# A two-layer attention encoder: three multiplications of branch attention placed on other engines

## The chip, the core and the metric

The kernel runs on one core of one Trainium2 chip. The core has TensorE (PE, matrix products into PSUM), VectorE (DVE), ScalarE (ACT), GpSimd (POOL) and SyncE (SP, which issues the weight loads). Each engine works through its own queue in order and waits on semaphores for the others. The metric is the device time of one execution in microseconds (us).

## The reference

A batch of one sequence of 512 tokens, width 1024, passes two equal layers. Cut to what matters here:

```python
h = rms_norm(x, norm_mix)
qa, ka, va, qb, kb, vb, qc, kc, vc, gate_logits = split(h @ w_in)
qa, ka = (apply_rope(rms_norm(t, gain), ang_1d) for t in (qa, ka))   # 4 heads of 64
qb, kb = (apply_rope(rms_norm(t, gain), ang_2d) for t in (qb, kb))   # 8 query heads, 2 key heads
qc, kc = rms_norm(qc, qk_gain[2, 0]), rms_norm(kc, qk_gain[2, 1])    # 4 heads, no rotation
oa = dilated_mixture_attention(qa, ka, va)        # softmax over masked scores
ob = gqa_block_attention(qb, kb, vb)              # softmax over all 512 keys
oc = neighborhood_attention_2d(qc, kc, vc, rpb)   # softmax over near keys, with a bias
merged = sum(sigmoid(gate) * (o @ w_branch))      # over the three branches
x = x + merged @ w_out
x = x + ffn(rms_norm(x, norm_ffn))                # up, depthwise conv, gelu gate, down
```

`apply_rope` makes `[x1 cos - x2 sin, x1 sin + x2 cos]` of the two halves of a head. The scores are scaled by 1/8.

## The kernel before, in words

All data is float32. A product of two float32 matrices is made of three passes on PE over high and low parts: a number is cast to the type fp32r (the high part, a cast on ACT) and the difference is the low part (a subtraction on DVE). Each weight granule (128 x 512) is loaded by SP and split in this way, `whi` on ACT at line 104 and `wlo` on DVE at line 106; three buffers of each are in turn. `mm3` (lines 117 to 120) makes the passes for outputs that stand feature by feature, `token_group` (lines 156 to 158) for outputs token by token. A granule feeds twelve matmuls.

A layer projects queries and keys of C (`Qc`), then the values, the keys of B (`Qk`) and the queries of B (`Qb`), gates, and later the queries and keys of A (`Qa`). `headnorm` normalises a projection head by head: squares on ACT, sums on DVE, a reciprocal root in a few small DVE steps, and a multiplication of each block of 128 tokens on DVE (line 302), after which `finish` runs. For A and B `finish` is `rotate`: two products of swapped halves with the sine table into `m` on POOL (line 316), a product with the cosine table (line 322) and a sum (line 325) on DVE. For C it is `gain_c`, a product with the gains on POOL (line 537). In A and B the gains are in the tables.

Attention works on one head and one block of 128 queries at a time. `turned` transposes two heads' queries or keys on PE (line 345), `q_stack` and `k_stack` make high and low parts of them (`qT`, `kh`, `kl`; lines 352, 353, 362, 364). `scores` multiplies (lines 378 and 379), takes the maximum on DVE (line 387, or with the bias added in line 390), the exponential and its sum on ACT (388 or 394), and on DVE the reciprocal of the sum (396) and the scaling of the probabilities `p` by it (397). `turn` transposes `p` on PE (409) and splits it, `th` on ACT (413) and `tl` on DVE (414). `values` multiplies by the values (426, 427). Three PSUM buffers are shared by scores, transposes and results of this part.

`weave` sets the attention steps of one branch between the projections and gates of the others, so that PE has matmuls to do while a block's chain runs on DVE and ACT: C's heads stand among the projections of values and `Qb`, B's among gates, C's output and `Qa`, A's among B's output and gates. The order within each engine's queue is made by a scheduler from the program's order and from priorities: `soon` and `urgent` put the chain and the copies out of PSUM ahead, `next_w` the splits of the weights ahead of both. The last part of a layer, output projection and feed-forward, has no attention in it.

## Time and profile before

| | |
|---|---|
| three runs, median (lowest to highest) | 1665.42 us (1664.78 to 1666.51) |
| the profiled execution, own time | 1666.58 us |
| its span, first to last instruction | 1664.8 us |
| TensorE's granted clock, mean over the span | 0.999 of full speed |
| PE busy | 1625.6 us (98%) |
| DVE busy | 1163.5 us (70%) |
| ACT busy | 782.5 us (47%) |
| POOL busy | 153.3 us (9%) |

The span of the profiled execution is what the views of the trace divide up; 1.8 us of its own time lie around it. A busy PE is not a PE at its peak, since matmuls overlap: one of 512 columns is shown as 0.39 us and the next starts 0.23 us after it. Idle time of PE is thus the time in which not even the tail of a matmul runs. `L397` is line 397 of the kernel; a buffer's name stands before the arrow and what it is made of behind it.

### The profile page before, as it was taken

The page shows a single profiled execution, that of the slowest core. Times are in us where ns is not written, and L with a number is a line of the kernel's source. Part 1 is how long each engine was busy: PE and PEld are TensorE (multiplying, and loading weights), DVE is VectorE, ACT ScalarE, POOL GpSimd, SP SyncE. Part 2 cuts the span into 40 slices and gives each one's busy share as a digit, 9 for nine tenths or more (in the row PEclk, how much of TensorE's full clock was granted, in tenths as well). Part 3 has the DMA queues.
Part 4 walks back from the last instruction along what each step waited for, and adds up shares of the span by engine and source line. Part 5 has one row for each costly group of instructions (what it writes and reads, how often), then busy time and mean ns, then how long its engine had stood idle before and what let it go on. Part 6 is the DMA issues. An engine that isn't in the chain of part 4 may idle for free.

```text
span 1664.8 us, 21596 instructions
## 1 busy us (share of the span) xinstructions
PE 1625.6 (98%) x7697; PEld 1340.9 (81%) x7697; DVE 1163.5 (70%) x2110; ACT 782.5 (47%) x1424; POOL 153.3 (9%) x150
## 2 busy tenths in 40 slices
PE   8999999999999999999999999999999999999999
PEld 6777888787888888888876778887878888888887
DVE  7898778866677734776388987788575677357753
ACT  5556565554454423444245566655543444234431
POOL 2220012203000000000031200122020000000000
PEclk9999999999999999999999999999999999999999
DMA  5222122222333333333332221222223333333333
GB/s 191 81 84 65 63 70 66 69 65 91 97 92 101 95 98 98 96 95 102 95 107 80 85 66 61 70 71 63 71 89 98 98 96 96 97 99 95 97 100 101
DMA packets 80092, 147.78 MB, mean 89 GB/s; under 512 B 8913, under 2 KB 10065, under 8 KB 79985
## 3 DMA queue, kind: packets, MB, share of 16 engines
q1 hardware_dynamic: 77184, 140.54, 27.3%
q10 hardware_dynamic: 2736, 5.74, 1.1%
q8 instruction: 60, 0.98, 0.2%
q14 instruction: 48, 0.39, 0.1%
q0 software_dynamic: 64, 0.12, 0.0%
HBM read 144.28 MB, written 2.10 MB: 88 GB/s over the span
## 4 chain that ended last, share of the span: by engine, by line
PE 84%; DVE 10%; issue 2%; ACT 2%; POOL 1%; DMA 1%; SPq 0%; DVEq 0%; ACTq 0%; POOLq 0%
PE acc L118 23%; PE acc L120 23%; PE acc L119 23%; PE acc L156 3%; PE acc L158 3%; PE acc L157 3%; DVE wlo L106 2%; PE tpp L409 2%; PE s L378 2%; PE s L379 1%; PE po L427 1%; PE po L426 1%; DVE p L397 1%; DVE tl L414 1%; DVE p L390 1%
## 5 line engine op out<-in xcount | busy, mean ns | idle before, releaser
L106 DVE TENSOR_TENSOR wlo<-raw,whi 128x512 fp32r<-128x512 f32 x520 | 378.6, 729 | 403.7 <-ACT whi L104 314.5
L104 ACT CAST whi<-raw 128x512 fp32r<-128x512 f32 x520 | 322.0, 620 | 556.8 <-PE acc L119 411.3
L118 PE MATMUL acc<-xh,whi 128*128 128x512 f32 x1152 | 452.3, 393 | 0.0
L120 PE MATMUL acc<-xh,wlo 128*128 128x512 f32 x1152 | 449.7, 390 | 0.0
L119 PE MATMUL acc<-xl,whi 128*128 128x512 f32 x1152 | 449.1, 390 | 0.0
L120 PEld LDWEIGHTS acc<-xh,wlo 128*128 128x128 f32 x1152 | 216.2, 188 | 45.4
L119 PEld LDWEIGHTS acc<-xl,whi 128*128 128x128 f32 x1152 | 216.4, 188 | 44.4
L118 PEld LDWEIGHTS acc<-xh,whi 128*128 128x128 f32 x1152 | 216.3, 188 | 43.7
L118 PE MATMUL acc<-gh,whi 128*128 128x512 f32 x384 | 149.4, 389 | 0.0
L119 PE MATMUL acc<-gl,whi 128*128 128x512 f32 x384 | 149.4, 389 | 0.0
L120 PE MATMUL acc<-gh,wlo 128*128 128x512 f32 x384 | 149.4, 389 | 0.0
L156 PE MATMUL acc<-whi,xh 128*128 128x512 f32 (+1 forms) x320 | 120.4, 378 | 4.1 <-ACT whi L104 1.5
L157 PE MATMUL acc<-wlo,xh 128*128 128x512 f32 (+1 forms) x320 | 119.5, 373 | 1.4 <-DVE wlo L106 1.4
L158 PE MATMUL acc<-whi,xl 128*128 128x512 f32 (+1 forms) x320 | 119.0, 372 | 0.7 <-DVE xl L186 0.7
L689 ACT ACTIVATE cv<-us,params 128x512 f32<-128x512 f32 x96 | 75.6, 811 | 31.8 <-DVE us L687 31.8
L413 ACT CAST th<-tpp 128x512 fp32r<-128x512 f32 (+2 forms) x128 | 69.7, 544 | 32.7 <-PE tpp L409 28.4
L118 PEld LDWEIGHTS acc<-gh,whi 128*128 128x128 f32 x384 | 72.1, 188 | 15.0
L120 PEld LDWEIGHTS acc<-gh,wlo 128*128 128x128 f32 x384 | 72.1, 188 | 15.0
L119 PEld LDWEIGHTS acc<-gl,whi 128*128 128x128 f32 x384 | 72.1, 188 | 14.9
L414 DVE TENSOR_TENSOR tl<-tpp,th 128x512 fp32r<-128x512 f32 (+2 forms) x128 | 81.0, 634 | 2.5 <-ACT th L413 1.9
L409 PE MATMUL tpp<-ident,p 128*128 128x128 f32 x464 | 72.9, 275 | 6.0 <-DVE tl L414 2.3
L156 PEld LDWEIGHTS acc<-whi,xh 128*128 128x128 f32 x320 | 60.7, 190 | 15.3 <-ACT whi L104 2.2
(149 smaller groups left out, 2339.4 us busy)
## 6 DMA issues: line engine op xcount, KB each, us to landing
raw<-w SPq DMA_DIRECT2D x520, 256.0 KB, 2.6
x_all<-xT SPq DMA_DIRECT2D x8, 256.0 KB, 5.4
bias_a<-bias_a ACTq DMA_DIRECT2D x4, 512.0 KB, 4.4
out<-x_all SPq DMA_DIRECT2D x8, 256.0 KB, 2.6
T<-rpb ACTq DMA_DIRECT2D x8, 192.0 KB, 2.8
rope_raw<-rope ACTq DMA_DIRECT2D x4, 256.0 KB, 3.7
gn<-gains ACTq DMA_DIRECT2D x2, 384.0 KB, 4.1
params<-small ACTq DMA_DIRECT2D x1, 232.0 KB, 4.0
```

Of the source, the lines that this page charges most:

```text
L104: nc.scalar.copy(hi, src)
L106: nc.vector.tensor_tensor(out=lo, in0=src, in1=hi.bitcast(F32), op=ALU.subtract)
L118: nc.tensor.matmul(ps, lhsT=lh, rhs=rh, start=first, stop=False)
L119: nc.tensor.matmul(ps, lhsT=lh, rhs=rl, start=False, stop=False)
L120: nc.tensor.matmul(ps, lhsT=ll, rhs=rh, start=False, stop=last)
L156: nc.tensor.matmul(o, lhsT=xh[:, t], rhs=wh[:, c], start=k == 0, stop=False)
L157: nc.tensor.matmul(o, lhsT=xh[:, t], rhs=wl[:, c], start=False, stop=False)
L158: nc.tensor.matmul(o, lhsT=xl[:, t], rhs=wh[:, c], start=False, stop=k == KD - 1)
L409: nc.tensor.transpose(tp[:, i * 128 : (i + 1) * 128], p[:, i * 128 : (i + 1) * 128], ident)
L413: nc.scalar.copy(hd["th"][sl], v_)
L414: nc.vector.tensor_tensor(out=hd["tl"][sl], in0=v_, in1=hd["th"][sl].bitcast(F32), op=ALU.subtract)
L689: nc.scalar.activation(out=t, in_=us, func=AF.Identity, scale=cw[:, 1, j : j + 1], bias=cb[:, j : j + 1])
```

## The change

Three things are done otherwise.

1. `gain_c` is gone. The small parameters get two more columns for each layer, the gains of C's queries and keys. One DVE call for each layer makes their product times -0.125 (`g_c`), and `q_stack` multiplies C's transposed queries by it while it splits them: ACT's copy gets a column of scales, DVE's subtraction becomes a multiply-and-subtract. The keys of C get no gain of their own any more.
2. In `rotate` the two products of swapped halves are made on DVE. There are 48 in the run: 32 of 128x256 for `Qa` and `Qb`, 16 of 128x64 for `Qk`.
3. The scaling of `p` by the reciprocal sum is an ACT copy with a column of scales. There are 128.

```diff
--- before.py
+++ after.py
@@ -22,7 +22,7 @@
 KF = DFF // 128
 EPS = 1e-6
 BIG = 1e30
-NSMALL = 3 * 48 + 48 + 24 + 8 + 8
+NSMALL = 3 * 48 + 48 + 24 + 8 + 8 + 2
 
 
 
@@ -243,6 +243,11 @@
         g_ffn = sm[:, 224:232]
         nc.vector.tensor_scalar(out=bg, in0=bg, scalar1=0.5, scalar2=None, op0=ALU.mult)
 
+        g_c = sm[:, 232:233]
+        nc.vector.scalar_tensor_tensor(
+            out=g_c, in0=g_c, scalar=-0.125, in1=sm[:, 233:234], op0=ALU.mult, op1=ALU.mult
+        )
+
         with ExitStack() as actx:
             at = actx.enter_context(tc.tile_pool(name=f"att{l}", bufs=1, reuse_waits="tile"))
             xh, xl, split = normed(x, g_mix, "A", res)
@@ -257,7 +262,7 @@
                     nc.scalar.dma_start(
                         out=gn.rearrange("p a b c d -> p (a b c d)"), in_=gains[l : l + 1, :].to_broadcast([128, 768])
                     )
-                for br, s in ((0, -0.125), (1, 0.125), (2, -0.125)):
+                for br, s in ((0, -0.125), (1, 0.125)):
                     nc.vector.tensor_scalar(
                         out=gn[:, br, 0], in0=gn[:, br, 0], scalar1=s, scalar2=None, op0=ALU.mult
                     )
@@ -313,7 +318,7 @@
                 mv = m[:, :w_].rearrange("p (s h d) -> p s h d", s=ns, d=64)
                 Qv = Q.rearrange("p (s h d) -> p s h d", s=ns, d=64)
                 for a, b in ((0, 32), (32, 0)):
-                    nc.gpsimd.tensor_tensor(
+                    nc.vector.tensor_tensor(
                         out=mv[:, :, :, a : a + 32],
                         in0=Qv[:, :, :, b : b + 32],
                         in1=table(1)[:, :, None, a : a + 32].to_broadcast([128, ns, nh, 32]),
@@ -345,12 +350,21 @@
                     nc.tensor.transpose(tp[:, b * 128 : (b + 1) * 128], Q[:, b, c : c + 128], ident)
                 return tp
 
-            def q_stack(tp, odd):
+            def q_stack(tp, odd, gain):
 
                 qT = at.tile([128, 512], F32R, tag="qT", bufs=3, name=nm("qT"))
                 src = tp[64 * odd : 64 * odd + 64, :]
-                nc.scalar.copy(qT[0:64], src)
-                nc.vector.tensor_tensor(out=qT[64:128], in0=src, in1=qT[0:64].bitcast(F32), op=ALU.subtract)
+                if gain is None:
+                    nc.scalar.copy(qT[0:64], src)
+                    nc.vector.tensor_tensor(out=qT[64:128], in0=src, in1=qT[0:64].bitcast(F32), op=ALU.subtract)
+                else:
+                    nc.scalar.activation(
+                        out=qT[0:64], in_=src, func=AF.Copy, scale=gain[64 * odd : 64 * odd + 64]
+                    )
+                    nc.vector.scalar_tensor_tensor(
+                        out=qT[64:128], in0=src, scalar=gain[0:64], in1=qT[0:64].bitcast(F32),
+                        op0=ALU.mult, op1=ALU.subtract,
+                    )
                 return qT
 
             def k_stack(tp, odd):
@@ -394,7 +408,7 @@
                         nc.scalar.activation(out=p, in_=p, func=AF.Exp, bias=m, scale=-1.0, accum_out=den)
                 with soon():
                     nc.vector.reciprocal(out=rden, in_=den)
-                    nc.vector.tensor_scalar(out=p, in0=p, scalar1=rden, scalar2=None, op0=ALU.mult)
+                    nc.scalar.activation(out=p, in_=p, func=AF.Copy, scale=rden)
                 hd["p", b] = p
 
             def turn(hd, b):
@@ -457,7 +471,7 @@
                     else:
                         tp = turned(pair[0]["Q"], pair[0]["qc"])
                         for i, hd in enumerate(pair):
-                            hd["qT"] = q_stack(tp, i)
+                            hd["qT"] = q_stack(tp, i, hd["gain"])
 
                 def slot(s):
                     nxt = s // 8 * 8 + 8
@@ -532,13 +546,7 @@
 
             Qc = at.tile([128, 4, 512], F32, tag="Q", bufs=2, name=nm("Qc"))
 
-            def gain_c(b):
-                v_ = Qc[:, b].rearrange("p (s h d) -> p s h d", s=2, d=64)
-                nc.gpsimd.tensor_tensor(
-                    out=v_, in0=v_, in1=gn[:, 2, :, 0][:, :, None, :].to_broadcast([128, 2, 4, 64]), op=ALU.mult
-                )
-
-            norm_c = headnorm(Qc, 8, gain_c)
+            norm_c = headnorm(Qc, 8, lambda b: None)
 
             def ev_c(b, ps):
                 copy_q(Qc[:, b], b, ps)
@@ -577,10 +585,10 @@
                 f = bc.rearrange("p k c -> p (k c)")
                 return lambda b: (f[:, 0:256], f[:, 256:640], f[:, 256:640], f[:, 640:896])[b]
 
-            def head(h, Q, qc, K, kc, v, vh, outs, blocks=lambda b: range(4), bias=None, prep=None):
+            def head(h, Q, qc, K, kc, v, vh, outs, blocks=lambda b: range(4), bias=None, prep=None, gain=None):
                 return dict(
                     h=h, Q=Q, qc=qc, K=K, kc=kc, v=v, vh=vh, outs=outs, blocks=blocks,
-                    bias=bias, bias_prep=prep,
+                    bias=bias, bias_prep=prep, gain=gain,
                 )
 
 
@@ -598,7 +606,7 @@
             oC = []
             near = lambda b: range(max(0, b - 1), min(4, b + 2))
             heads_c = [
-                head(h, Qc, h * 64, Qc, 256 + h * 64, vC, h, oC, blocks=near, prep=lambda h=h: bias_c(h))
+                head(h, Qc, h * 64, Qc, 256 + h * 64, vC, h, oC, blocks=near, prep=lambda h=h: bias_c(h), gain=g_c)
                 for h in range(4)
             ]
             gC, gate_c = gates(2)
@@ -837,6 +845,7 @@
                 per(b_gate),
                 per(norm_mix),
                 per(norm_ffn),
+                np.concatenate([qk_gain[:, 2], qk_gain[:, 2]], axis=2).transpose(2, 0, 1),
             ],
             axis=2,
         )
```

By the added lines, lines 302, 316, 322 and 325 become 307, 321, 327 and 330; 353 becomes 364 for branch C; 390, 394, 396, 397, 413 and 414 become 404, 408, 410, 411, 427 and 428. Numbers in names only tell buffers apart, and differ by a few between the two programs.

The first place is DVE's queue in the first layer at the third block of C's first head, where its probabilities (`p_735` before; its sum's reciprocal is `rden_734`, and `rden_730` after) become ready. Before:

```order
L390 ISA p_752,m_749<-s_746,bc_534 128x256
L390 ISA m_749 128x1
L396 RECIPROCAL rden_734<-den_733 128x1
L198 TENSOR_SCALAR nx_616<-hss_183 128x8
L353 TENSOR_TENSOR qT_563<-tpq_555,qT_563 64x512
L106 TENSOR_TENSOR wlo_925<-raw_921,whi_923 128x512
L397 TENSOR_SCALAR p_735<-p_735,rden_734 128x384
L396 RECIPROCAL rden_751<-den_750 128x1
L199 TENSOR_SCALAR rq_184<-nx_616 128x8
L397 TENSOR_SCALAR p_752<-p_752,rden_751 128x256
```

Now:

```order
L404 ISA p_748,m_745<-s_742,bc_530 128x256
L404 ISA m_745 128x1
L410 RECIPROCAL rden_730<-den_729 128x1
L198 TENSOR_SCALAR nx_612<-hss_184 128x8
L199 TENSOR_SCALAR rq_185<-nx_612 128x8
L202 TENSOR_SCALAR rq_185<-rq_185 128x8
L106 TENSOR_TENSOR wlo_921<-raw_917,whi_919 128x512
L204 TENSOR_TENSOR nt_613<-rq_185 128x8
L205 SCALAR_TENSOR_TENSOR nt_613<-nt_613,nx_612 128x8
L206 SCALAR_TENSOR_TENSOR rq_185<-nt_613,rq_185 128x8
L410 RECIPROCAL rden_747<-den_746 128x1
```

The scalings of `p` have left this queue, and the reciprocal for the block after it still stands behind the `wlo` (`rden_751` before, `rden_747` now), while the one for this block keeps its place ahead of it.

The second place is ACT's queue at the same blocks (`p_735` before is `p_731` now). Before:

```order
L394 ACTIVATE p_735,den_733<-p_735,m_732 128x384
L104 CAST whi_923<-raw_921 128x512
L394 ACTIVATE p_752,den_750<-p_752,m_749 128x256
L564 DMA T_1102<-rpb 128x384
L413 CAST th_782<-tpp_784 128x3x128
L394 ACTIVATE p_796,den_794<-p_796,m_793 128x256
L104 CAST whi_967<-raw_965 128x512
L413 CAST th_782<-tpp_819 128x2x128
```

Now:

```order
L408 ACTIVATE p_731,den_729<-p_731,m_728 128x384
L104 CAST whi_919<-raw_917 128x512
L411 ACTIVATE p_731<-p_731,rden_730 128x384
L408 ACTIVATE p_748,den_746<-p_748,m_745 128x256
L572 DMA T_1098<-rpb 128x384
L411 ACTIVATE p_748<-p_748,rden_747 128x256
L427 CAST th_778<-tpp_780 128x3x128
L408 ACTIVATE p_792,den_790<-p_792,m_789 128x256
L411 ACTIVATE p_792<-p_792,rden_791 128x256
L104 CAST whi_963<-raw_961 128x512
L427 CAST th_778<-tpp_815 128x2x128
```

Behind each exponential there is now a scaling that needs the reciprocal from DVE, in two places with nothing between them, and `whi` and `th` stand behind it.

The third place is DVE's queue at the normalising and the rotation of the first two blocks of `Qb`. Before:

```order
L302 TENSOR_TENSOR Qb_185<-Qb_185,rq_187 128x512 x2
L396 RECIPROCAL rden_1196<-den_1195 128x1
L106 TENSOR_TENSOR wlo_1336<-raw_1332,whi_1334 128x512
L397 TENSOR_SCALAR p_1197<-p_1197,rden_1196 128x256
L414 TENSOR_TENSOR tl_1184<-tpp_1220,th_1183 128x2x128
L322 TENSOR_TENSOR Qb_185<-Qb_185,rope_246 128x512 x2
L390 ISA p_1231,m_1228<-s_1225,bc_1104 128x384
L390 ISA m_1228 128x1
L106 TENSOR_TENSOR wlo_1359<-raw_1355,whi_1357 128x512
L325 TENSOR_TENSOR Qb_185<-Qb_185,m_1048 128x512
```

Now:

```order
L307 TENSOR_TENSOR Qb_186<-Qb_186,rq_188 128x512 x2
L321 TENSOR_TENSOR m_1044<-Qb_186,rope_246 128x8x32
L428 TENSOR_TENSOR tl_1180<-tpp_1181,th_1179 128x3x128
L321 TENSOR_TENSOR m_1044<-Qb_186,rope_246 128x8x32
L321 TENSOR_TENSOR m_1050<-Qb_186,rope_246 128x8x32
L106 TENSOR_TENSOR wlo_1332<-raw_1328,whi_1330 128x512
L404 ISA p_1193,m_1190<-s_1187,bc_1100 128x256
L404 ISA m_1190 128x1
L327 TENSOR_TENSOR Qb_186<-Qb_186,rope_246 128x512
L321 TENSOR_TENSOR m_1050<-Qb_186,rope_246 128x8x32
L410 RECIPROCAL rden_1192<-den_1191 128x1
L428 TENSOR_TENSOR tl_1180<-tpp_1216,th_1179 128x2x128
```

The products into `m` now stand in this queue between the normalising and the cosine products, ahead of a `wlo` and of the maximum of a block of scores (line 390, now 404). On POOL the same rows are gone, and nothing else of POOL's order has changed; SP's order is the same.

## Rows read from the trace of the kernel before

**Rows 1.** The page, part 1: busy time, share, instructions by engine.

```profile
PE 1625.6 (98%) x7697; PEld 1340.9 (81%) x7697; DVE 1163.5 (70%) x2110; ACT 782.5 (47%) x1424; POOL 153.3 (9%) x150
```

**Rows 2.** Busy time by stretch: length, PE, PEld, DVE, ACT, POOL, granted clock, DMA share, GB/s.

```profile
56.00:145.00 89.00, 80.62 (x400) 62.67 (x399) 81.78 (x205) 53.67 (x121) 18.19 (x24) 1.00 0.24 76
145.00:240.00 95.00, 95.00 (x510) 80.71 (x509) 73.93 (x141) 55.53 (x112) 2.59 (x2) 1.00 0.21 64
240.00:350.00 110.00, 105.82 (x579) 88.44 (x578) 91.64 (x176) 58.96 (x117) 26.75 (x23) 1.00 0.22 68
880.00:985.00 105.00, 96.36 (x475) 75.70 (x474) 91.91 (x222) 62.23 (x137) 18.39 (x24) 0.98 0.24 73
```

**Rows 3.** Who PE waited for, 56 to 145 us: total us, times, longest.

```profile
PE s L378 <- DVE tl L414: 2.2, 4, 0.8
PE s L378 <- DVE qT L353: 1.5, 2, 0.9
PE tpp L409 <- DVE p L397: 1.4, 1, 1.4
PE acc L156 <- ACT Qk L530: 1.0, 1, 1.0
```

**Rows 4.** Timeline at 106 us (start, us; idle before), POOL, DVE, PE picked out.

```profile
106.13 4.04 POOL L316 TENSOR_TENSOR m<-Qb,rope 128x256 f32<-128x256 f32 x4 [15.67 <-ACT p L394]
...
106.55 1.16 DVE L106 TENSOR_TENSOR wlo<-raw,whi 128x512 fp32r<-128x512 f32 x1
107.64 0.82 DVE L397 TENSOR_SCALAR p<-p,rden 128x256 f32<-128x256 f32 x1
...
107.37 0.39 PE L119 MATMUL acc<-xl,whi 128*128 128x512 f32 x1
107.60 0.40 PE L120 MATMUL acc<-xh,wlo 128*128 128x512 f32 x1
108.84 0.44 PE L378 MATMUL s<-kh,qT 128*128 128x384 f32 x1 [0.84 <-DVE tl L414]
```

**Rows 5.** DVE groups (busy us, mean ns): 145 to 240, 56 to 145, 240 to 350.

```profile
L106 DVE TENSOR_TENSOR wlo<-raw,whi 128x512 fp32r<-128x512 f32 x22 | 15.2, 691 | 9.9 <-ACT whi L104 6.8 <-PE tpp L409 2.8
L397 DVE TENSOR_SCALAR p<-p,rden 128x512 f32<-128x512 f32 x23 | 11.2, 486 | 0.6
...
L106 DVE TENSOR_TENSOR wlo<-raw,whi 128x512 fp32r<-128x512 f32 x21 | 17.3, 825 | 2.3 <-ACT whi L104 2.1
L397 DVE TENSOR_SCALAR p<-p,rden 128x384 f32<-128x384 f32 x8 | 4.3, 538 | 0.0
L397 DVE TENSOR_SCALAR p<-p,rden 128x256 f32<-128x256 f32 x8 | 3.9, 488 | 0.0
L397 DVE TENSOR_SCALAR p<-p,rden 128x512 f32<-128x512 f32 x3 | 1.5, 487 | 0.1
...
L397 DVE TENSOR_SCALAR p<-p,rden 128x512 f32<-128x512 f32 x19 | 12.5, 660 | 0.4
```

**Rows 6.** Groups of the whole run, DVE and ACT, each shape apart.

```profile
L302 DVE TENSOR_TENSOR Qc<-Qc,rq 128x512 f32<-128x512 f32 x8 | 9.5, 1231 | 0.1
L325 DVE TENSOR_TENSOR Qk<-Qk,m 128x128 f32<-128x128 f32 x8 | 2.1, 281 | 0.0
...
L184 ACT ACTIVATE xh<-x_all,params 128x512 fp32r<-128x512 f32 x16 | 11.4, 717 | 2.7 <-DVE x_all L723 2.7
L331 ACT ACTIVATE vA<-acc,rcol 128x256 fp32r<-128x256 f32 x8 | 3.3, 466 | 0.0
```

**Rows 7.** Timeline of PE in the second layer at 872 us.

```profile
872.72 0.50 PE L157 MATMUL acc<-wlo,xh 128*128 128x512 f32 x1 [1.12 <-DVE wlo L106]
```

**Rows 8.** Line 397 of the whole run: who waited for it.

```profile
  PE tpp L409: 2.1, 2
```

**Rows 9.** The reciprocal of the whole run, as in rows 5.

```profile
L396 DVE RECIPROCAL rden<-den 128x1 f32<-128x1 f32 x128 | 20.5, 160 | 23.1 <-ACT p L388 12.7 <-ACT p L394 9.3
```

**Rows 10.** Who PE waited for, 240 to 350 us, as in rows 3.

```profile
PE s L378 <- ACT p L388: 1.0, 2, 0.5
```

## The prediction

> **What bounds the kernel now.** I read the page first: TensorE (PE) is busy for 98% of the span, VectorE (DVE) for 70%, ScalarE (ACT) for 47%, GpSimd (POOL) for 9% [rows 1]. A kernel of that shape gets faster only where PE stands idle, so the second view is the busy time by stretch [rows 2]. In 56 to 145 us (branch C's heads among the projections of the first layer) PE is busy for 80.62 of 89 us, so 8.38 us idle; its twin in the second layer (880 to 985) has 8.64 us idle; where branch B ends and A starts (240 to 350) it is 4.18 us, and I take as much for that place in the second layer. In pure branch B (145 to 240) there is none. The stretches with idle PE are those in which POOL works most and DVE is fullest: 81.78 of 89 us in the first, against 73.93 of 95 in B.
>
> Third, what PE waits for in 56 to 145 us [rows 3]: mostly DVE, namely `tl` (the low halves of the probabilities, whose end frees a PSUM buffer for the next scores), `qT`, and once the scaled probabilities `p`; ACT once, for a copy of `Qk`. A look at one such wait [rows 4] shows how it comes about. POOL runs four swapped products of the rotation for 4.04 us from 106.13. In that time DVE's `wlo` takes 1.16 us and a 256-wide scaling of `p` 0.82 us, and the scores that wait behind them start at 108.84. The last matmul before them started at 107.60, and matmuls else start 0.23 us apart, so this wait costs 1.01 us where the idle column says 0.84. I take every microsecond of PE's idle time as 1.2 us of span.
>
> Without that company `wlo` takes 691 ns (mean in branch B), with it 825 ns (mean in 56 to 145 us) [rows 5]. So POOL's work costs DVE time, and DVE's lateness costs PE time.
>
> **The gain on the query and key of C.** The change takes away POOL's multiplication of `Qc` by the gains (8 calls in all) and puts the product of both gains into the query stack. Beside those calls DVE's normalising of `Qc` takes 1231 ns [rows 6], about 0.54 us over an undisturbed 691 ns [rows 5], 4.3 us for the 8. PE pays for it at one place: in the second layer it waits 1.12 us for a `wlo` queued behind them [rows 7], 1.3 us by the factor above. Nothing of the kind stands in the first layer, where the projection's matmuls cover it; without that cover the same 1.3 us would be due there. The stack's new forms (a copy with a column of scales, a multiply-and-subtract) replace calls of the same size, eight pairs in the run; I put nothing on them, bounded by 0.1 us each way a call, 1 us in all. The two column products at the start stand before the first `xl` on DVE: 0 to 0.4 us, taken as 0.2. Together: -1.1 us.
>
> **The rotation.** 48 products leave POOL for DVE: 32 of 128x256 and 16 of 128x64. The trace has none on DVE. Its nearest rows are 281 ns for a 128x128 sum from SBUF [rows 6] and 691 ns for 128x512 [rows 5]; these bound the wide ones, and a line through both gives 418 ns, and 212 ns for the narrow ones (bounds 0 and 281). The C stretch holds eight of each: 3.3 + 1.7 = 5.0 us more on DVE. What DVE gets back is POOL's disturbance: 21 `wlo` at 134 ns over 691 are 2.8 us, and the eight wide products are 8 of POOL's 18.2 us there, so 1.3 us. DVE no longer waits for POOL inside a rotation, but behind the products in DVE's queue stand `wlo`, the maxima and `tl`, for which PE waits.
>
> [rows 4] shows a POOL call of about 1 us lengthening `wlo` by 0.47 us, not by its whole length. The Trainium skill, "SBUF — State Buffer" (Who interferes with whom), says that a GpSimd call and a VectorE call with two SBUF inputs exclude each other on a shared port pair for the whole instruction. By that rule DVE would get back 8 us in such a stretch and not 1.3, and the sum would be 1651; this is the third rival below.
>
> **The scaling of the probabilities.** 128 calls go from DVE to ACT. In 56 to 145 us they are 4.3 + 3.9 + 1.5 = 9.7 us of DVE [rows 5], in 240 to 350 us 12.5 us [rows 5]. On ACT the nearest row is a 128x512 copy with a column of scales from SBUF to SBUF, 717 ns [rows 6]; a 256-wide one from PSUM takes 466 ns [rows 6]. I take 717 for 512 columns and about 0.54 on average for C's 256 and 384; a block's chain gets longer by 0.23 us and a hand-over, 0.3 us. That is covered almost everywhere: of 128 scalings PE waited for two [rows 8]. If the cover were gone in all 128 it would be 38 us.
>
> The order on DVE shows one more thing: at the third block of C the scaling stood behind a `wlo`, the reciprocal ahead of it. Now only the reciprocal is needed from DVE. The wait of 1.4 us for `p` [rows 3] is the wait of that place.
>
> **The sum for PE.** How PE's waits answer to a freer DVE no row tells. I assume that idle time falls as DVE's free time grows (a queue's waits go roughly with one over its slack); bounds are nothing and all of it. In C's first stretch DVE's busy time becomes 81.8 - 9.7 + 5.0 - 1.3 = 75.8 of 89 us; the free time grows from 7.2 to 13.2, and PE's idle time falls by 45%, 3.8 us. In the second layer the same 6.0 us come off 91.9 of 105; free 13.1 becomes 19.1; 31%, 2.7 us. From B into A it is 91.6 - 12.5 + 3.3 = 82.4 of 110 (POOL's relief left out); free 18.4 becomes 27.6; 33%, 1.4 us, and as much in the second layer.
>
> That is 9.3 us idle, 11.2 us of span by the factor 1.2. Left out is TensorE's clock: its granted mean is 0.98 of full speed in C's second stretch and 1.00 in the others [rows 2]; if the shorter waits kept it up, some 2 us more would come (2% of 105), if they moved a drop into a fuller place, as much would go.
>
> Against it stands ACT. In C it takes 16 scalings at 0.54 (8.6 us) and waits in its queue for 16 reciprocals. One takes 0.16 us, and DVE stands idle 23.1/128 = 0.18 us before it [rows 9], so 0.34 us each, 5.4 us. ACT's free time of 35.3 us becomes 21.3. By the same rule PE's 1.0 us of waiting for ACT [rows 3] grows by 0.7. In B into A 19 scalings and their waits (13.6 + 6.5 us) leave 30.9 of 51.0 us, and the 1.0 us of waiting there [rows 10] grows by 0.65 in each layer. That is 2.0 us, 2.4 with the factor, and 2 x 0.3 us for the two waits for `p`: +3.0 us. Behind the waiting scaling on ACT stand `whi`, `th` and the exponentials; PE and DVE wait for these. The loads of C's bias tables are issued there too and come as much later, a head ahead of their use.
>
> In branch B the sum is 0: PE has no idle time, DVE loses 23 scalings [rows 5], and ACT goes from 55.5 [rows 2] by 23 x 0.717 to about 72 of 95 us. The merges, the feed-forward part and the DMAs aren't touched.
>
> Sum: -1.1 - 11.2 + 3.0 = -9.3 us. The profiled execution took 1666.58 us (span 1664.8 and 1.8 around it), which gives 1657.3; it was 1.2 us over the median of the runs, 1665.42, so 1656.1, rounded to 1656 us.
>
> **The rivals.** The first: ACT becomes the engine that is late, and it is slower. Each block puts 0.717 us of scaling and 0.34 us of waiting, 1.06 us, ahead of the next `th` on ACT, and `tl` follows `th`. There are some 70 blocks in the four stretches. The relief of 12.3 us (1.1 + 11.2) is used up when 12 of them reach PE; with 16 it is 17 - 12.3 = 4.7 us slower, 1670. For it: in a stretch where DVE is over 90% busy ACT waits longer than 0.34 us for a reciprocal. Against it: ACT still has 21 us free there, and 126 of 128 had slack. The Trainium skill, "ScalarE: Activation LUTs" (Rules for kernel authors), says to multiply on VectorE and not on ScalarE; the 717 against 486 ns agree with it as to the call, and by it the move alone costs. Chance 0.14.
>
> The second, hidden: PE's waits are for `tl`, and `tl` comes no earlier because `th` on ACT comes later by what DVE gains. Then only the 1.3 us at `Qc` and the 1.4 us for `p` (1.7 with the factor) go, and some 1 us comes back: 1666.6 - 2.0 - 1.2 = 1663.4. For it: DVE is 78% busy in branch B without idle PE and 83% in 240 to 350 us with 4.18 us of it [rows 2], so fullness alone isn't the cause. Chance 0.14.
>
> The third: POOL's company cost DVE its whole length, eight calls of about 1 us [rows 4]. DVE gets back 8 us a stretch: C falls to 69.0 of 89 (idle less by 64%, 5.4 us), C again to 79.1 of 105 (49%, 4.3 us), B into A to 74.4 of 110 (48%, 2.0 us, twice). That is 13.7 x 1.2 = 16.4 us, and with the other two terms -14.5: 1666.6 - 14.5 - 1.2 = 1651. With all waits on DVE gone (25.4 us idle less 3.0 that are for ACT, times 1.2, 26.9 us) it would be 1666.6 - 1.1 - 26.9 + 3.0 - 1.2 = 1640. Chance 0.11.
>
> **How the numbers follow.** My forecast (1652 to 1662) gets 0.61. What a measurement of this kernel can tell from no change is about 0.2%, 3.3 us. Faster by more: forecast, third rival and a little of the second, 0.75. Within: most of the second, 0.11. Slower: the first, 0.14. The range 1644 to 1669 reaches over the second rival and into the third.
>
> **What would show it.** Right: in 56 to 145 us DVE near 76 us and PE's idle time near 5 us; `wlo` under 800 ns; POOL without products of the rotation; ACT near 62 us there with few PE waits named after it; no change in branch B or the feed-forward part. Wrong: rows in which PE waits for `whi` or `th`, or ACT for `rden` by 1 us and more (first rival); `tl` still the longest wait with DVE idle before it (second); new idle PE in branch B.

## The result and the profile after

| | us, median (lowest to highest) | ratio to before, 95% interval |
|---|---|---|
| before, four runs beside the changed kernel | 1665.97 (1664.78 to 1667.41) | |
| changed | 1642.80 (1641.03 to 1645.22) | 0.9861 (0.9848 to 0.9873) |
| forecast | 1656 (1644 to 1669) | |

The change is 23.2 us faster. The sign was right, the gain was two and a half times the 9.3 us forecast, and the time lies just under the range.

The page of the changed kernel, part 1 (busy time by engine) and the first line of the chain that ended last (share of the span by engine):

```profile
PE 1617.5 (99%) x7697; PEld 1339.9 (82%) x7697; DVE 1097.5 (67%) x2030; ACT 854.6 (52%) x1552; POOL 103.2 (6%) x94
...
PE 91%; DVE 4%; ACT 2%; issue 1%; POOL 1%; DMA 0%; SPq 0%; ACTq 0%; DVEq 0%; POOLq 0%
```

The work went where the diff sent it: 66 us off DVE, 72 onto ACT, 50 off POOL against [rows 1]. PE's idle time (span 1639.3 less busy 1617.5) is 21.8 us; before it was 1664.8 less 1625.6, 39.2 us. So 17.4 us of idle time went, and 25.5 us of span: 1.47 for one, not the 1.2 of the forecast. (The profiled execution is the fastest of the changed kernel's four, so its gain is a little over the 23.2 us of the medians.) Some 2 us of the 25.5 are TensorE's clock: its granted mean is 0.98 in C of the second layer in [rows 2], over 105 us, and 1.00 there now. The forecast had named these 2 us and left them out; without them it is about 1.35 for one.

Busy time by stretch in the changed kernel (columns as in [rows 2]; the stretches end 5 to 15 us earlier, since the kernel is ahead by then):

```profile
56.00:140.00 84.00, 80.09 (x400) 62.52 (x399) 75.65 (x202) 62.38 (x140) 8.28 (x8) 1.00 0.24 78
140.00:235.00 95.00, 95.00 (x512) 80.19 (x512) 63.38 (x117) 69.04 (x135) 2.59 (x2) 1.00 0.20 64
235.00:345.00 110.00, 109.49 (x605) 93.62 (x604) 85.72 (x176) 74.55 (x143) 18.12 (x15) 1.00 0.24 73
870.00:970.00 100.00, 95.76 (x487) 76.31 (x487) 85.29 (x220) 74.23 (x162) 7.89 (x8) 1.00 0.25 77
```

PE's idle time in C falls from 8.38 to 3.91 us, in C again from 8.64 to 4.24, and from B into A from 4.18 to 0.51. The reader should see DVE's column beside it: 75.65 of 84 us is 90%, hardly less than the 92% of [rows 2], and yet half of the waits are gone. From B into A DVE is still 78% busy and nearly all of them are gone. The waits did not go in step with DVE's load, as the forecast had assumed they would.

Who PE waits for in the first stretch, 56 to 140 us of the changed kernel (total us, times, longest):

```profile
PE acc L156 <- ACT Qk L544: 1.2, 1, 1.2
PE s L392 <- DVE tl L428: 1.0, 3, 0.5
PE tpq L350 <- DVE rden L410: 0.7, 1, 0.7
```

Against [rows 3] the waits for `tl` are half and those for `qT` nearly gone, the 1.4 us for `p` too; the one for ACT's copy of `Qk` stayed. Instruction groups of the same stretch (count, busy us, mean ns, idle time of the engine before them):

```profile
L106 DVE TENSOR_TENSOR wlo<-raw,whi 128x512 fp32r<-128x512 f32 x21 | 14.4, 688 | 2.2 <-ACT whi L104 1.9
L411 ACT ACTIVATE p<-p,rden 128x384 f32<-128x384 f32 x8 | 4.9, 611 | 0.3 <-DVE rden L410 0.3
L411 ACT ACTIVATE p<-p,rden 128x256 f32<-128x256 f32 x8 | 4.1, 507 | 3.6 <-DVE rden L410 3.5
L321 DVE TENSOR_TENSOR m<-Qb,rope 128x256 f32<-128x256 f32 x8 | 3.2, 420 | 0.0
L411 ACT ACTIVATE p<-p,rden 128x512 f32<-128x512 f32 x3 | 2.2, 722 | 0.0
```

The prices of the calls were right: 420 ns for a swapped product (418 forecast), 722 for a 512-wide scaling (717), 0.56 us for C's two shapes (0.54), `wlo` back at 688 ns. So the error is not in what a call takes.

The signs that the forecast had named for being right came as well: DVE at 75.65 us, PE idle for 3.91, `wlo` at 688 ns, ACT at 62.38 us, no idle time in branch B. One sign of its first rival came too: over the run ACT waits up to 2.1 us for a reciprocal (line 411 for 410). None of them could tell what follows.

### The profile page after: what moved, and what is told of

Its sections match the earlier page's. It is cut to its first block, busy times and chain, and to the rows that moved or that the text cites. A ratio compares the mean times of both kernels' runs of the same rounds, so it can differ in the third digit from the quotient of the medians.

```text
span 1639.3 us, 21606 instructions
## 1 busy us (share of the span) xinstructions
PE 1617.5 (99%) x7697; PEld 1339.9 (82%) x7697; DVE 1097.5 (67%) x2030; ACT 854.6 (52%) x1552; POOL 103.2 (6%) x94
## 4 chain that ended last, share of the span: by engine, by line
PE 91%; DVE 4%; ACT 2%; issue 1%; POOL 1%; DMA 0%; SPq 0%; ACTq 0%; DVEq 0%; POOLq 0%
PE acc L118 24%; PE acc L120 24%; PE acc L119 24%; PE tpp L423 3%; PE acc L156 3%; PE acc L158 3%; PE acc L157 3%; PE s L392 2%; PE po L441 2%; PE po L440 2%; PE s L393 1%; DVE wlo L106 1%; ACT whi L104 1%; PE tpq L350 1%; DVE p L404 0%
## 5 line engine op out<-in xcount | busy, mean ns | idle before, releaser
L106 DVE TENSOR_TENSOR wlo<-raw,whi 128x512 fp32r<-128x512 f32 x520 | 364.2, 701 | 433.8 <-ACT whi L104 345.3
L411 ACT ACTIVATE p<-p,rden 128x512 f32<-128x512 f32 (+2 forms) x128 | 87.3, 683 | 19.1 <-DVE rden L410 16.8
```

Source lines behind the costliest of these rows:

```text
L106: nc.vector.tensor_tensor(out=lo, in0=src, in1=hi.bitcast(F32), op=ALU.subtract)
L411: nc.scalar.activation(out=p, in_=p, func=AF.Copy, scale=rden)
```

## The experiments

Each one is compared with runs of the kernel before on the same chip; the median of these lay between 1665.97 and 1666.88 us. "Moved work" is the scaling and the swapped products; the gain of C is a small third part.

### The three parts alone

The first theory, D, was that DVE's queue is shorter, mostly by the scaling; the rival, P, that POOL's company was the larger part. The scaling alone:

```diff
-                    nc.vector.tensor_scalar(out=p, in0=p, scalar1=rden, scalar2=None, op0=ALU.mult)
+                    nc.scalar.activation(out=p, in_=p, func=AF.Copy, scale=rden)
```

> The kernel before with the scaling of the probabilities on ScalarE and nothing else changed. Theory D (PE's waits came from the length of VectorE's queue, and the 128 scalings that leave it are the larger part of the gain of 23 us): 1649 to 1653 us, 13 to 17 us under the kernel before. Rival P (GpSimd's calls holding up VectorE are the larger part): 1658 to 1662 us. If ScalarE were the engine that is late: 1666 us or more.

The rotation's products alone:

```diff
-                    nc.gpsimd.tensor_tensor(
+                    nc.vector.tensor_tensor(
                         out=mv[:, :, :, a : a + 32],
```

> The kernel before with the rotation's swapped products on VectorE and nothing else changed. Theory D: 1660 to 1665 us, since VectorE gets 5 us of calls in a stretch of C and gets back little more than that. Rival P: 1648 to 1653 us.

The gain alone (the changed kernel with the other two parts put back):

> The kernel before with the gains of C applied in the query stack and nothing else changed. Both theories: 1664 to 1666 us, the one wait of 1.3 us in the second layer and no more.

Measured: scaling 1655.06 (0.9932, 0.9918 to 0.9947), rotation 1654.62 (0.9931, 0.9916 to 0.9946), gain 1664.03 (0.9987, 0.9978 to 0.9997). The rotation gives as much as the scaling, 11.8 against 11.3 us, though it puts 16 us of products onto DVE; the scaling alone fell between the numbers of both theories, and the rotation alone fell below D's. D as it stood was refuted, and P was not confirmed either. The parts add up (25.5 us against 23.2), which looked like three independent gains and was not, as the later runs show: each of the three kernels also has queues in an order of its own (against the kernel before, PE's differs in 112, 87 and 56 places).

### Company and load put back

POOL's company on the changed kernel: the same products, from the rotated block, into a tile that nobody in the attention reads.

```diff
                 nc.vector.tensor_tensor(out=Q, in0=Q, in1=m[:, :w_], op=ALU.add)
+                sv = x[2][:, :w_].rearrange("p (s h d) -> p s h d", s=ns, d=64)
+                for a, b in ((0, 32), (32, 0)):
+                    nc.gpsimd.tensor_tensor(
+                        out=sv[:, :, :, a : a + 32],
+                        in0=Qv[:, :, :, b : b + 32],
...
```

The products spoil the third residual tile, an input of later stages.

> The changed kernel with GpSimd making products of the same number, sizes and places as the rotation's before, on the rotated block, into a part of the input that is not needed until the end of attention; nobody waits for them. (The output is not the reference's, since that part of the residual input is written over.) It gives back GpSimd's company without VectorE's wait for it. Theory D: 2 to 5 us over the changed kernel. Rival P: 10 us and more over it.

Measured: 1646.85, 4.05 us over the changed kernel. The same lines on the kernel with the rotation alone:

> The rotation alone on DVE (1654.6 us), with POOL making products of the same number and size from the rotated block into the third residual tile (which they spoil), and nobody waiting for them. Scaling stays on DVE. Theory C (the move of the rotation gives its 11.8 us because POOL's calls no longer lengthen DVE's beside them): most of it goes, 1662 to 1666. Rival W (it gives them because DVE's queue and the chain behind a rotation no longer stand until POOL, whose product takes 1.0 us against 0.42, is done): 2 to 4 us go, as in the run with company on the changed kernel, 1656 to 1659.

Measured: 1659.64, 5.0 us over the rotation alone; rival W's side, a little above its numbers. No run with the company overlaps one without it. So company is worth 4 to 5 us, not 12. In both, the queues of PE, DVE and ACT kept their order.

DVE's load put back, and ACT's load added to the kernel before:

```diff
+                    nc.vector.tensor_scalar(
+                        out=x[2][:, :n], in0=x[2][:, :n], scalar1=rden, scalar2=None, op0=ALU.mult
+                    )
```

> The changed kernel, with one more in-place multiply by the reciprocal sum on DVE behind each of the 128 reciprocals, of the size of the probabilities block but on the third residual tile (which it spoils: that input of the later stages is left wrong), so nobody in the attention waits for it. ACT keeps the real scaling. DVE's busy time should go from 1097.5 to about 1157 us. Theory Q (what the scaling's move gives is that DVE's queue is 60 us shorter): the time goes back by what the scaling alone gave, 8 to 11 us, to 1651 to 1654. Rival L (what it gives is the chain: a block's probabilities no longer stand behind other work of DVE): 0 to 2 us, 1643 to 1645.

Measured: 1647.27. DVE's busy time rose by 54 us to 1151.4 and the kernel lost 4.5 us. Neither theory had that. (Its queues were in another order too; the section on other orders comes back to it.)

```diff
                     nc.vector.tensor_scalar(out=p, in0=p, scalar1=rden, scalar2=None, op0=ALU.mult)
+                    nc.scalar.activation(out=x[2][:, :n], in_=x[2][:, :n], func=AF.Copy, scale=rden)
```

> The kernel before, with one more in-place scaling by the reciprocal sum on ACT behind each of the 128 on DVE, on the third residual tile (which it spoils), so ACT gets the change's 72 us and its waits for the reciprocals while DVE is not relieved. ACT's busy time should go from 781 to about 853 us. Theory (ACT has room in every stage, the counter term of 3.0 us was put too high): 0 to 2 us slower, 1666 to 1668. Rival (ACT is late when it scales, the price of the forecast's first rival): 5 to 10 us slower, 1671 to 1676.

Measured: 1657.25 (0.9942, 0.9925 to 0.9960), **9 us faster** with 73 us more work on ACT and nothing taken from anyone. Theory and rival were both wrong here. The added calls touch nothing on PE, but the scheduler that makes each queue's order answered them: listed side by side, PE's queue stands in another order in 97 places, and DVE's queue differs in 145. Between the gain alone and the changed kernel PE's queue differs in 119 places. Third theory, O: the new order of the queues is a large part of the change.

### The order alone, the work alone

To part them, the order that the scheduler gave to one kernel was written down and imposed on the calls of another, as edges between neighbours on an engine that cost no semaphore:

```diff
+def pin(nc, tc):
+    for engine, packed in ORDER.items():
+        steps = np.frombuffer(zlib.decompress(base64.b64decode(packed)), np.int16)
...
+        q = [rows[j] for j in np.cumsum(steps)]
+        for a, b in zip(q, q[1:]):
+            tc.add_manual_dep(
+                b, a.name, mybir.DependencyInfo(mybir.DependencyClass.NoSync, mybir.DependencyReason.SCHED_ONLY)
+            )
...
         encoder(tc, **args)
+        pin(nc, tc)
```

`ORDER` is the written-down order by engine, `rows` the engine's calls as the program makes them. Where two kernels have a call on different engines (scaling, swapped products), it is left out of the table, and the scheduler places it. In the traces the calls of PE, DVE and ACT that are in the table stand in exactly the order of the kernel that it was taken from (for the first and the third of the other orders below that kernel has no trace). The added lines move the kernel's lines down by five: `tl` of line 414 is at 419, or at 433 where the changed kernel has it at 428. First a control:

> A control: the kernel before with its own order written down and imposed in the same way as in the runs with another order. Every theory: no change, ratio to before 0.998 to 1.002, some 1664 to 1669 us. Were it faster by several us, the imposing itself would be part of what the other runs show.

Measured: 1665.97 (0.9996, 0.9987 to 1.0005): imposing costs and gives nothing that these runs can tell. Then the four corners of the ACT run:

> The kernel before with nothing added and nothing moved to another engine, but each engine's queue in the order that the scheduler gave to the kernel with the extra scaling on ACT (which ran in 1657.3 us, 9 us under before, though it only has more to do). That order is written down and imposed on PE, DVE, ACT and POOL; the extra calls are left out of it. Theory O (the order of the queues is what made that kernel faster): 1654 to 1659. Rival E (the calls themselves did, by holding ACT back): 1665 to 1668, as before.

> The other corner: the kernel before with the 128 extra scalings on ACT of the third residual tile (which they spoil), all other calls of PE, DVE, ACT and POOL in the order of the kernel before. Theory O (the order made it faster, and the calls only cost): 1666 to 1672. Rival E (the calls themselves make it faster): 1656 to 1659.

Measured: 1656.36 (0.9941, 0.9926 to 0.9956) for the unchanged calls in the other order, and 1673.45 (1.0041, 1.0026 to 1.0055) for the extra calls in the old one. The order alone is worth 10.3 us; the same ACT calls cost 6.8 us in the old order and 0.9 in the order made for them, which is within the measurement. Theory O held in both; the second cost more than it had said.

Then the same for the change itself:

> The calls of the kernel with the gain alone changed (1664.0 us: scaling on DVE, swapped products on POOL), with all calls on PE, DVE and ACT but these two kinds in the order that the scheduler gave to the changed kernel; the two kinds are placed by the scheduler. Theory O (a good half of the change's 21 us over the gain alone is the order): 1646 to 1654. Rival E (it is the work taken off the engines, and the order is worth nothing without it): 1662 to 1668.

> The calls of the changed kernel, with all on PE, DVE and ACT but the scalings and the swapped products in the order of the kernel with the gain alone changed (1664.0 us). Theory O: the moved work alone gives less than half, 1653 to 1661. Rival E: the moved work gives nearly all, 1642 to 1648.

| | order of the gain alone | order of the changed kernel |
|---|---|---|
| calls of the gain alone | 1664.03 | 1656.79 (0.9941, 0.9926 to 0.9956) |
| calls of the changed kernel | 1660.23 (0.9963, 0.9948 to 0.9978) | 1642.80 |

The order alone gives 7.2 us, a little less than theory O had said, the moved work in the old order 3.8 us, as it had said; both together give 21.2, that is 10.2 us more than the sum. By the intervals of the ratios each of the differences is sure to some 3 us, and the 10.2 to some 4. The table can be read either way round: in the new order the moved work gives 14.0 us. So the 10.2 us belong to neither alone. Busy time by stretch of three corners, from B into A in the second layer: the gain alone, its calls in the new order, the changed calls in the old order:

```profile
1055.00:1165.00 110.00, 105.98 (x581) 88.61 (x580) 93.00 (x177) 59.18 (x117) 25.45 (x22) 1.00 0.22 68
```

```profile
1055.00:1165.00 110.00, 109.04 (x600) 92.36 (x599) 91.95 (x182) 61.34 (x120) 26.23 (x23) 1.00 0.23 70
```

```profile
1055.00:1165.00 110.00, 107.30 (x585) 90.07 (x585) 83.81 (x167) 72.08 (x138) 18.21 (x15) 1.00 0.23 70
```

With DVE as full as before (92 of 110 us) the order alone takes PE's idle time from 4.02 to 0.96 us; with DVE relieved by 9 us, but in the old order, 2.70 us stay. The forecast's rule gives 2.6 for that (4.02 times 17.00 over 26.19 us of DVE's free time), so here it holds as long as the order stays. In C of the second layer it doesn't, the gain alone and then the changed calls in the old order:

```profile
870.00:970.00 100.00, 92.56 (x455) 72.38 (x453) 84.96 (x209) 58.29 (x129) 19.95 (x24) 1.00 0.27 81
```

```profile
870.00:970.00 100.00, 92.42 (x461) 72.37 (x460) 81.31 (x211) 70.44 (x154) 7.85 (x8) 1.00 0.27 79
```

DVE has 3.65 us more free, and PE is idle for 7.58 us instead of 7.44. In branch B, where the forecast had put nothing, the old order leaves PE idle for 0.92 us (140 to 235 us), in one wait for `qT`. The two profiled executions lie 7.3 us apart in span, further than the medians.

The two moves apart, in the order of the kernel before:

> The scaling alone on ACT, with all other calls of PE, DVE and ACT in the order of the kernel before. With an order of its own it gave 11.3 us. Theory O (most of that was its order; PE's idle time is set by what stands ahead in the queues): 1661 to 1667, that is 0 to 5 us under before. Rival E (the relief of DVE by 60 us is the gain and needs no other order): 1655 to 1658.

> The rotation's products alone on DVE, with all other calls of PE, DVE and ACT in the order of the kernel before. With an order of its own it gave 11.8 us. Theory O: 1661 to 1666. Rival E (POOL's company and DVE's waits for POOL are the gain): 1654 to 1657. With the run before, this says whose relief the 3.8 us of both in the old order are.

Measured: scaling 1661.11 (0.9966, 0.9953 to 0.9979), 5.5 us; rotation 1665.82 (0.9995, 0.9986 to 1.0004), no change. The scaling landed on the edge of theory O's numbers, the rotation in them. So about half of the scaling's 11.3 us and nearly all of the rotation's 11.8 come only together with the order made for them. What those orders give without the moved calls was not run.

What an order does can be read at one place. Timeline at 81 us of the rotation on DVE in the old order (start, us, engine, line; idle time before it):

```profile
80.94 0.39 PE L162 MATMUL acc<-wlo,xh 128*128 128x512 f32 x1
80.94 0.29 DVE L327 TENSOR_TENSOR Qk<-Qk,rope 128x128 f32<-128x128 f32 x1
81.16 0.68 DVE L369 TENSOR_TENSOR kl<-tpq,kh 64x512 fp32r<-64x512 f32 x1
81.76 0.41 DVE L419 TENSOR_TENSOR tl<-tpp,th 128x256 fp32r<-128x256 f32 x1
...
82.21 0.45 PE L383 MATMUL s<-kh,qT 128*128 128x384 f32 x1 [0.89 <-DVE tl L419]
```

and of the same calls in their own order:

```profile
81.08 0.39 PE L157 MATMUL acc<-wlo,xh 128*128 128x512 f32 x1
81.20 0.42 DVE L414 TENSOR_TENSOR tl<-tpp,th 128x256 fp32r<-128x256 f32 x1
81.53 0.28 DVE L322 TENSOR_TENSOR Qk<-Qk,rope 128x128 f32<-128x128 f32 x1
81.67 0.19 PEld L378 LDWEIGHTS s<-kh,qT 128*128 128x128 f32 x1 [0.63 <-DVE tl L414]
81.67 0.44 PE L378 MATMUL s<-kh,qT 128*128 128x384 f32 x1 [0.20 <-DVE tl L414]
```

In the old order a `kl` (the low half of the keys of B, 0.68 us) stands ahead of the `tl` for which PE waits; in the new one it doesn't. From the last projection matmul to the next scores it is 1.27 us in the old order and 0.59 in the new one: one call of DVE, shifted in its queue. DVE has no less to do. PE's waits for attention in that whole stretch, 56 to 140 us, old order and then own order (those of the scores for `tl`, and the two longest single ones that the second lacks):

```profile
PE s L383 <- DVE tl L419: 1.5, 3, 0.9
PE tpp L414 <- DVE o L440: 1.3, 1, 1.3
PE tpp L414 <- DVE m L395: 1.2, 1, 1.2
```

```profile
PE s L378 <- DVE tl L414: 0.5, 2, 0.2
```

At the same scores the changed kernel gets there by another way. Its calls in the old order, and then in their own:

```profile
80.58 0.40 PE L163 MATMUL acc<-whi,xl 128*128 128x512 f32 x1
81.66 0.45 PE L397 MATMUL s<-kh,qT 128*128 128x384 f32 x1 [0.68 <-DVE tl L433]
```

```profile
81.24 0.39 PE L157 MATMUL acc<-wlo,xh 128*128 128x512 f32 x1
81.82 0.44 PE L392 MATMUL s<-kh,qT 128*128 128x384 f32 x1 [0.19 <-DVE tl L428]
```

Here DVE ends `tl` no earlier, and a `kl` stands right ahead of it in DVE's new queue; but in PE's own queue two more matmuls of the projection now stand ahead of the scores. From start to start it is 1.08 us in the old order and 0.58 in the new one.

### Other orders for the changed kernel

Does the changed kernel's own order fit best? Its calls in the orders that the scheduler makes when one more scaling on ACT, one more multiplication on DVE, or two more scalings on ACT stand behind each reciprocal (the extra calls themselves left out):

> The changed kernel, all its calls and no others, in the order that the scheduler gives to the changed kernel with one more scaling on ACT for each block (the trick that took 10 us off the kernel before). Theory: the scheduler sees chains that are too short, and an order made for a longer one leaves PE less to wait for here too: 1637 to 1641. Rival: the changed kernel's own order fits its calls, another one doesn't: 1644 to 1652.

> The changed kernel, all its calls and no others, in the order that the scheduler gives to it with one more multiplication on DVE for each block (that kernel itself ran in 1647.3 us with 54 us more work on DVE). Theory (that order would fit a DVE that is later than the scheduler thinks): 1638 to 1641. Rival (no gain, the kernel's own order fits better): 1643 to 1648.

> The changed kernel, all its calls and no others, in the order that the scheduler gives to it with two more scalings on ACT for each block instead of one (one gave 1638.3 us). Theory (the longer the modelled chain, the further apart score and transpose stand, and PE's waits shrink on): 1634 to 1637. Rival (there is a best length; beyond it the blocks run out of work between them and PE waits at the end of a stretch): 1639 to 1646.

Measured: 1638.30 (1637.97 to 1639.11; 0.9831, 0.9817 to 0.9846), 1643.68 (0.9867, 0.9850 to 0.9883) and 1666.58 (0.9996, 0.9987 to 1.0005). The first is faster than both kernels, by 4.5 us over the changed one, and no run of the one overlaps a run of the other; the second is level with the changed kernel, and against it DVE's 54 us of the load run, in the same order, cost 3.6 us, hardly more than the measurement can tell; the third gives the whole gain of the change back with not one call different. C in the second layer of the first of them:

```profile
870.00:970.00 100.00, 97.68 (x496) 78.08 (x497) 84.88 (x219) 73.90 (x158) 8.79 (x8) 1.00 0.27 82
```

PE is idle for 2.32 us there (4.24 in the changed kernel), DVE as busy as ever. Of the third, who PE waits for most (whole run), and 1080 to 1120 us by engine:

```profile
PE tpq L355 <- DVE Qa L335: 8.5, 5, 2.5
```

```profile
1080.00:1120.00 40.00, 33.61 (x212) 29.37 (x212) 32.76 (x70) 23.36 (x46) 4.95 (x5) 0.94 0.19 59
```

PE comes to the transposes of A's rotated block up to 2.5 us before DVE has it. Rival "there is a best length" held, with more lost than it had said.

### The last additions on DVE

```diff
-            run(branch_out(oA, 2, gA, False))
+            run(branch_out(oA, 2, gA, False, nc.vector))
```

(the last argument is the engine that adds into the merged sum)

> The changed kernel, with the eight additions of each layer's last branch into the merged sum on DVE instead of POOL, where PE waits 1.47 us for the last of them behind a POOL call of 1.29 to 1.49 us. Theory (the last call is the chain: DVE does it in about 0.7 us): 0.7 us a layer, 1641 to 1642. Rival (DVE is the one that is late there, and its queue gets 8 calls longer): 1643 to 1646.

Measured: 1652.28, 9.5 us slower than the changed kernel, worse than the rival had said; PE's order is the same but for ten places. PE's waits in 345 to 410 us, and the merge of the second layer by engine:

```profile
PE acc L118 <- DVE gate L530: 2.4, 1, 2.4
PE acc L119 <- DVE ml L663: 1.9, 1, 1.9
```

```profile
1165.00:1225.00 60.00, 55.75 (x245) 45.30 (x244) 34.12 (x58) 25.33 (x45) 1.29 (x1) 0.94 0.25 75
```

The adds, the gates and `ml` now stand behind one another on DVE; PE waits 4.3 us where the changed kernel has one wait of 1.3, in each layer, and the granted clock falls to a mean of 0.94 in that stretch, in the first layer to 0.97 over 345 to 410 us (1.00 in both in the changed kernel). Two engines side by side were worth more there than the faster engine alone.

## Why the prediction was off

**Which step failed.** "I assume that idle time falls as DVE's free time grows." Around it the sum moved single calls and left every queue's order as [rows 3] and [rows 4] show it. But the order is made by the scheduler from the whole program, and it was made anew. Of the 21.2 us that the moved work gave over the gain alone, 3.8 came in the old order (by the intervals 1 to 7); the other 17.4 came only together with the new one, which by itself gave 7.2 with DVE as full as before. The sum had 8.2 us for these two parts (11.2 less 3.0): by the medians more than twice what the work alone gives, and less than half of what came. Two errors of different sign met, so the forecast was not even as near as it looks. In the old order the assumption is right from B into A and wrong in C of the second layer and in branch B, as the lines above show; that PE's idle time is set by DVE's free time alone is what the order run refutes.

**The rotation.** The prices of its calls held, but in the old order the move is worth nothing (0.8 us, within the measurement): DVE takes 16 us of products, and POOL's company, worth 4 to 5 us, goes. The forecast's reading of [rows 4], that POOL's work costs DVE time and this costs PE time, was right in kind.

**The scaling.** 5.5 us in the old order. That it pays although ACT takes 722 ns for what DVE did in 486 goes against the rule that the forecast had weighed (the Trainium skill, "ScalarE: Activation LUTs", Rules for kernel authors: multiply on VectorE). The trace bears the rule out for the call and not for the kernel.

**ACT's counter term.** Forecast +3.0 us. In the changed kernel ACT waits 0.33 us for a reciprocal where it waits (16.8 us, 51 waits; 0.34 forecast), but extra scalings of the same size cost 6.8 us in the old order and 0.9 in their own. So 3.0 is too small for what such calls cost in the old order; what the term is in the changed kernel's own order no run shows. The first rival (ACT late) has a base in that: load on ACT costs PE time in the old order. But the waits it named, for `whi` and `th`, didn't grow there: PE's one wait for `whi` is 1.6 us with the extra calls and 1.5 before, while its waits for `qT` go from 5.9 to 7.8.

**The gain of C.** Forecast -1.1, measured -2.4 (interval 0.5 to 3.7 us); `Qc`'s normalising went from 1231 to 688 ns, and the wait of [rows 7] fell from 1.12 to 0.2 us. Right within the measurement, though not clean: PE's queue is in another order in 56 places there, and in the run of the gain alone a new wait of 1.9 us for ACT's copy of `Qc` stands near the old one (0.7 in the changed kernel).

**The factor 1.2** came from one wait and was 1.47 over the run, about 1.35 without the clock. What a wait hides under the tail of the matmul before it doesn't show in the idle column: at 81 us above, 0.20 us idle stands for 0.59 us between two starts that are else 0.23 us apart, so 0.36 us are lost. In so short a wait more is hidden than shown. That is a size, not a mechanism.

**Third rival** (POOL's company costs its whole length). Refuted: on the changed kernel 47.6 us of POOL's products, put back, lengthened DVE's busy time from 1097.5 to 1102.7 us, a ninth of their length. That the measured time lies near the 1640 that this rival had for all waits on DVE gone is chance: the order did it. The second rival (hidden) fell with the waits for `tl`: the scores' waits for it are 8.4 us in the gain alone, 4.8 with the moved calls in its order and 2.2 in the changed kernel.

**What stays open.** Which of the 119 places carries how much; one of them was shown, besides one of the rotation alone. How good the places are that the scheduler gave the moved calls in the old order, since it was free in these. And whether it is one queue's order or only that of all three together that counts: they were always imposed together.

## What to carry to other kernels

Where a scheduler makes the order, a moved call is two changes: its price and a new order of everything. Look at whether the bound engine's queue moves before pricing the change in the old order (the count of places does not tell the size: the second of the other orders differs from the changed kernel's in 110 places of PE's queue and is level with it), and widen the range by what an order is worth (here up to 28 us with the same calls). When a change gives an unexplained gain, impose the old order on the new calls and the new order on the old ones: the four corners tell work from order. A good order is a gain by itself: one made for slightly longer chains took 10 us off the kernel before and 4.5 off the changed one; one made for still longer chains took the whole gain back, so each has to be run.

## What the runs showed of the hardware

- POOL's calls beside DVE cost far less than the forecast made of them: 5.2 us of DVE's busy time for 47.6 us of POOL's on the changed kernel, where nobody waits for POOL's products. The trace of that run shows why. Only some of DVE's calls are stretched: `gate` made from `acc` in PSUM takes 668 to 689 ns in all 32 calls, 24 of them beside a POOL call, while `wlo` from two tiles in SBUF takes 673 to 1841. And POOL's calls are stretched too: its products on `Qa` take 727 to 3378 ns, 1759 in the mean (times on POOL are rough). This agrees with the rule that the forecast had cited (the Trainium skill, "SBUF — State Buffer", Who interferes with whom: a GpSimd call that reads SBUF contends with a VectorE call with two SBUF inputs); what failed was to charge DVE with POOL's whole length.
- Load on an engine with room is not free: 73 us more on ACT, which is about half busy, cost 6.8 us in the order of the kernel before. In the order made for them the same calls cost 0.9, within the measurement, and 54 us more on DVE in one order cost 3.6, hardly beyond it.
- Two waits in a merge cost more than their length. In the second layer's merge on DVE PE waited 2.4 and 1.9 us, and the granted clock's mean over these 60 us was 0.94; with one wait of 1.3 us it stayed at 1.00. The clock has two levels, 1.2 and 2.4 GHz, so 0.94 is about 7 us at the lower one, a loss of 3.6 us.
